# A two-layer attention and pooling step on one core: all low parts of weights on VectorE, layer 1's V tile behind the u tiles, new planner costs, queries by halves

## The chip, the cores and the metric

The kernel runs on one core of one Trainium2 chip. The metric is the device time of one execution in microseconds. A core has five engines that work side by side, each through its own queue of instructions in order: TensorE (PE) for matmuls and transposes, VectorE (DVE), ScalarE (ACT), GpSimd (POOL), and SyncE (SP), whose queue starts all transfers between memory and the on-chip buffer. An instruction that needs another engine's result waits for a semaphore, and what stands behind it in the same queue waits with it.

## The reference: one step of two layers

1152 tokens (128 context, 1024 latent) of width 1024 go through two layers. Each normalises and modulates the tokens, projects them with one matrix of width 2304, feeds a branch of windowed attention (8 query heads, 2 key and value heads) and a branch of pooling, gates both, and projects back into the residual. Results are the tokens after a last normalisation, and the context's keys and values.

```python
h = _rmsnorm(x, norm_w) * (1.0 + scale) + shift
p = h @ w_in
q, k, v, ga, u, gp = split(p)
# latent tokens: q = _rope_2d(q), k = _rope_2d(k); keys within 128 positions and all cached keys
s = jnp.einsum("bqkgd,bnkd->bkgqn", qb, k) * (HEAD_DIM ** -0.5)
m = jnp.maximum(jnp.max(s, -1), sink); e = jnp.exp(s - m)
p = e / (jnp.sum(e, -1) + jnp.exp(sink - m));  attn = p @ v
# pooling: four groups, means over windows of 2, 4, 8, 16, minus the token, then a 128 x 128 map
a = _rmsnorm(attn, attn_norm) * silu(ga);  pl = _rmsnorm(pool, pool_norm) * silu(gp)
x = x + gate * (concat(a, pl) @ w_out)
```

## The kernel before, in words

Tokens lie along the free dimension, in three groups of 384 (G0 to G2; the first 128 of G0 are the context). Channels lie in tiles of 128 partitions. Values that have to be exact to more than one pass of the matrix unit are split: a high part (a rounding copy) and a low part (value minus high part). So a *job* of the input projection, one tile of 128 output channels for one group, is 24 matmuls of 128 x 384: for each of 8 channel tiles weight high by h high, weight high by h low, weight low by h high (`project`). There are 18 such column tiles in a layer (4 q, K, V, 4 gates ga, 4 u, 4 gates gp) and 8 of the output projection, which are loaded twice, once for groups 0 and 1 (pass 1) and once for group 2. That makes 68 column tiles of weights.

Weights come in halves of 256 KB on SP (`wload`), into two raw buffers (`wr`, in the output projection's second pass parts of the tile R). `wsplit` then makes each half's high part on ScalarE and its low part on GpSimd, except for the first three tiles (`WDVE`) and the first half of each tile of the second pass, which are VectorE's. The results lie in two tiles `wh`; the next tile is split when all three groups of the one two before it have been multiplied.

The order within a layer is a list: u0, u1, V, u2, u3, K, q0 to q3, gp0 to gp3, ga0 to ga3, the same in both layers. Layer 0 runs the first three tiles of it as six lanes while its inputs arrive; layer 1 runs the first two for groups 0 and 1, then for group 2, then the rest tile by tile. Two PSUM accumulators (`acc`) take the jobs in turn, and each is evacuated by a routine of its kind. `evac_u` copies u into R, two u tiles at a time, where VectorE forms moving sums (`pool_group`); u2 may be written only when the sums of u0 are done, u3 after u1. When the sums of all four are done, SP loads the tables of cosines and sines over the same place of R (`pool_mix`), and these are needed by the rope of K and q (`evac_k`, `rope`). `evac_v` transposes V and splits it.

Attention runs as two lanes over 18 units (9 blocks of 128 queries, 2 key heads). A unit copies its four heads into the tile `qs` (high parts: heads 0 and 2 from the lower, heads 1 and 3 from the upper partitions, each also to the other half of partitions), subtracts for `ql` (low parts), multiplies with the stacked keys into PSUM tiles `pst`, takes row maxima on VectorE into `s`, exponentials on ScalarE, scales by 1/sum on GpSimd, transposes on TensorE, splits the result in `pth` (ScalarE) and `ptl` (VectorE) and multiplies with V into `pv`. The jobs of the later column tiles are run in between.

The order in each queue is no engine's choice at run time: a planner (`Sched`) runs the kernel's routines as generators against a model of time, always steps the ready routine of the highest priority, and issues instructions in that order. `Engine.cost` and `Tensor.matmul` say what an instruction is planned to take, `LAT` what a result needs to be seen by another engine, and `ready` and `commit` keep when each region of a tile was last written and read. The lines of the profile L111, L137, L148 and L160 are those of the helpers through which every instruction goes (engines, matmul, transpose, DMA), so groups are told apart by tile names.

## Time and profile before

| | us |
|---|---|
| median of 3 runs (range) | 972.14 (969.76 to 972.52) |
| the profiled execution | 972.32 |
| its span, first to last instruction | 970.5 |
| TensorE, VectorE, ScalarE, GpSimd busy | 919.0, 710.6, 533.1, 404.2 |
| mean granted TensorE clock, share of full | 0.993 |

The span is what the trace covers; the execution's own time has 1.8 us more around it. Busy is the time in which an engine has an instruction in work; a matmul's record overlaps the next one's, since they are pipelined. Start times in the views are counted from the span's start.

### The profile page before, as it was taken

To read this page: it belongs to the slowest core of one execution; us is meant where nothing else is said; L and a number is where in the kernel's file an instruction comes from. 1 tells how busy PE (TensorE), PEld (TensorE's weight loads), DVE (VectorE), ACT (ScalarE), POOL (GpSimd) and SP (SyncE) were. 2 spreads that over 40 slices of the span, in tenths; PEclk is the share of its full clock that TensorE was granted. 3 is DMA by queue.
4 is the path that set the end of the run, shared out by engine and by line. 5 is a ranking of instruction groups with operands and counts; after the bars stand their busy time and mean duration, and the time that the engine had idled before them with its cause. 6 is when DMAs were issued, how large, how long until landed. Compare 5 with 4: busy or idle time off the path is not lost.

```text
span 970.5 us, 15980 instructions
## 1 busy us (share of the span) xinstructions
PE 919.0 (95%) x5576; PEld 853.9 (88%) x5576; DVE 710.6 (73%) x1629; ACT 533.1 (55%) x1279; POOL 404.2 (42%) x419
## 2 busy tenths in 40 slices
PE   6899999999999999999989998999999999899995
PEld 2677787999999998899989998988999999899995
DVE  4876567788887569866797466888897776985675
ACT  3453334457766677653455433446776657875442
POOL 2142246663343354345333323776345326434331
PEclk9999999999999999999999999999999999999998
DMA  9714775010000010335431202000000001213463
GB/s 350 296 55 158 233 252 193 23 39 29 22 23 23 23 32 18 120 112 182 169 125 57 75 25 89 23 33 33 24 22 23 23 23 45 71 49 104 137 201 136
DMA packets 42560, 89.02 MB, mean 92 GB/s; under 512 B 4976, under 2 KB 7664, under 8 KB 42480
## 3 DMA queue, kind: packets, MB, share of 16 engines
q1 hardware_dynamic: 42480, 88.00, 26.4%
q8 instruction: 44, 0.72, 0.3%
q14 instruction: 36, 0.29, 0.1%
HBM read 78.28 MB, written 9.70 MB: 91 GB/s over the span
## 4 chain that ended last, share of the span: by engine, by line
PE 69%; DVE 18%; issue 5%; POOL 3%; ACT 3%; DMA 1%; SPq 0%; POOLq 0%; DVEq 0%; ACTq 0%
PE acc L137 46%; PE pst L137 10%; PE pst L148 7%; PE pv L137 6%; DVE G L111 5%; DVE H L111 3%; DVE t L111 2%; DVE R L111 2%; DVE s L111 2%; ACT s L111 1%; DVE ql L111 1%; DMA G<-in_xT 1%; POOL wh L111 1%; DVE den L111 1%; POOL t L111 1%
## 5 line engine op out<-in xcount | busy, mean ns | idle before, releaser
L137 PE MATMUL acc<-H,wh 128*128 128x384 f32 x3624 | 689.9, 339 | 16.2 <-DVE H L111 9.8
L137 PEld LDWEIGHTS acc<-H,wh 128*128 128x128 f32 x3624 | 633.1, 189 | 42.9 <-DVE H L111 12.2
L111 POOL TENSOR_TENSOR wh<-wr,wh 128x512 fp32r<-128x512 f32 x98 | 134.6, 1386 | 174.3 <-ACT wh L111 165.9
L111 POOL TENSOR_SCALAR s<-s,den 128x512 f32<-128x512 f32 (+2 forms) x144 | 105.3, 746 | 140.3 <-DVE den L111 76.9
L111 DVE TENSOR_TENSOR ptl<-pst,pth 128x512 fp32r<-128x512 f32 x124 | 82.4, 686 | 24.1 <-PE pv L137 14.3
L111 DVE CUSTOM_DVE_ANT_0 s<-pst,cst 128x512 f32<-128x512 f32 (+2 forms) x144 | 84.5, 613 | 13.3 <-PE pst L137 12.7
L111 ACT ACTIVATE s<-s,m 128x512 f32<-128x512 f32 (+2 forms) x144 | 93.9, 655 | 0.6
L111 ACT CAST wh<-wr 128x512 fp32r<-128x512 f32 x100 | 61.0, 616 | 54.9 <-PE acc L137 38.8
L111 ACT CAST pth<-pst 128x512 fp32r<-128x512 f32 x124 | 69.2, 585 | 32.5 <-PE pst L148 21.2
L148 PE MATMUL pst<-cst,s 128*128 128x128 f32 x504 | 70.5, 274 | 6.9 <-POOL s L111 5.3
L148 PEld LDWEIGHTS pst<-cst,s 128*128 128x128 f32 x504 | 59.3, 140 | 14.1 <-POOL s L111 8.9
L137 PE MATMUL pst<-K,ql 128*128 128x256 f32 x272 | 69.2, 283 | 1.0 <-DVE ql L111 0.9
L137 PE MATMUL pst<-K,qs 128*128 128x256 f32 x272 | 69.2, 283 | 0.0
L111 ACT ACTIVATE t<-G 128x384 f32<-128x384 f32 x86 | 43.7, 520 | 44.0 <-DVE G L111 28.1
L111 DVE TENSOR_TENSOR R<-R 128x384 f32<-128x384 f32 (+13 forms) x60 | 43.3, 722 | 25.9 <-ACT R L111 24.5
L111 ACT CAST qs<-G 64x256 fp32r<-64x256 f32 x144 | 58.2, 404 | 2.6
L111 DVE SCALAR_TENSOR_TENSOR G<-acc,mods,G 128x384 f32<-128x384 f32 (+2 forms) x64 | 31.5, 512 | 33.8 <-PE acc L137 33.5
L137 PEld LDWEIGHTS pst<-K,ql 128*128 128x128 f32 x272 | 51.3, 189 | 3.4 <-DVE ql L111 1.8
L137 PEld LDWEIGHTS pst<-K,qs 128*128 128x128 f32 x272 | 51.4, 189 | 0.3
L137 PE MATMUL pv<-ptl,V 128*128 128x512 f32 x124 | 50.2, 419 | 0.0
L111 POOL TENSOR_TENSOR rr<-rr,nhalf 128x3 f32<-128x3 f32 x21 | 21.5, 1026 | 68.6 <-DVE rr L111 68.3
L111 ACT COPY t<-pv 64x256 f32<-64x256 f32 x72 | 23.2, 369 | 47.0 <-PE pv L137 46.2
(125 smaller groups left out, 1206.2 us busy)
## 6 DMA issues: line engine op xcount, KB each, us to landing
wr<-in_wi SPq DMA_DIRECT2D x68, 256.0 KB, 2.6
s<-in_wada SPq DMA_DIRECT2D x44, 256.0 KB, 4.3
wr<-in_wo SPq DMA_DIRECT2D x32, 256.0 KB, 2.7
R<-in_wo SPq DMA_DIRECT2D x32, 256.0 KB, 3.8
wk<-in_wada SPq DMA_DIRECT2D x12, 512.0 KB, 7.8
G<-in_xT SPq DMA_DIRECT2D x6, 768.0 KB, 9.5
G<-in_xT SPq DMA_DIRECT2D x12, 384.0 KB, 3.9
xs<-G SPq DMA_DIRECT2D x12, 384.0 KB, 2.4
```

Of the source, the lines that this page charges most:

```text
L111: r = f(*args, **kw)
L137: self.eng.matmul(out, lhsT, rhs, start=start, stop=stop)
L148: self.eng.transpose(out, in_, ident)
```

## The change

Four things, all in the program that builds the kernel; the numbers computed are the same.

- `WDVE` becomes all tiles, so every low part of a weight is VectorE's: 114 halves move there from GpSimd.
- Layer 1 gets an order of its own: u0, u1, u2, u3, V, K, ... Layer 0 keeps its own.
- The planner's costs change: other durations by operation and operand, a time after the end until the result counts as written (`TAIL`, `DRAIN`), less `LAT` on top, a cost for switching between matmuls, transposes and matmuls on 32 columns, 35 ns between dependent instructions of one engine, and a port: GpSimd instructions, and VectorE instructions without a PSUM operand, are not planned at the same time.
- In `qs` and `ql` the two middle dimensions change places: heads 0 and 2 are now one contiguous half, heads 1 and 3 the other.

```diff
@@ -91,18 +91,35 @@
         self.sched, self.eng, self.name = sched, eng, name
         self.free = 0.0
 
+    TAIL = dict(act=105, dve=82, pool=45)
+    HOLD = dict(dve=50, pool=95)
+
     def cost(self, op, n, args, kw):
+        aps = [x for x in list(args) + list(kw.values()) if isinstance(x, bass.AP)]
+        psum = any(x.space == bass.MemoryType.PSUM for x in aps)
+        column = any(free_size(x) == 1 for x in aps if x is not args[0] and x is not kw.get("accum_out"))
         if self.name == "act":
-            return (205 if "accum_out" in kw else 107) + 0.763 * n
-        if self.name == "dve":
+            c = 280 + 0.83 * n if "accum_out" in kw else (80 + 0.755 * n if psum else 73 + 0.855 * n) + 100 * column
+        elif self.name == "dve":
             if op == "reciprocal":
-                return 70 + 6.6 * n
-            if op == "tensor_scalar" and not any(isinstance(x, bass.AP) and x.space == bass.MemoryType.PSUM for x in args):
-                return 70 + 0.52 * n
-            return 70 + 1.04 * n
-        if op == "tensor_tensor" and kw.get("op") == ALU.pow:
-            return 400 + 165 * n
-        return 70 + {"tensor_tensor": 2.35, "scalar_tensor_tensor": 1.46}.get(op, 1.2) * n
+                c = 70 + 6.6 * n
+            elif op == "tensor_reduce":
+                c = 50 + 1.05 * free_size(aps[1])
+            elif op == "memset":
+                c = 15 + 0.52 * n
+            elif op == "tensor_scalar" and not psum:
+                c = 80 + 0.52 * n
+            elif op == "stream_shuffle":
+                c = 190 + 1.05 * n
+            else:
+                c = 65 + 1.05 * n + (62 if column and op == "scalar_tensor_tensor" else 0)
+        elif kw.get("op") == ALU.pow:
+            c = 360 + 165 * n
+        elif op == "tensor_tensor":
+            c = 138 + 2.165 * n
+        else:
+            c = 225 + 0.865 * n
+        return c, self.name == "pool" or self.name == "dve" and not psum and op != "memset"
 
     def __getattr__(self, op):
         f = getattr(self.eng, op)
@@ -114,9 +131,14 @@
             ins += [v for k, v in kw.items() if isinstance(v, bass.AP) and k not in self.OUTS]
             s = self.sched
             start = max(self.free, s.clock, s.ready(ins, outs, self.name))
-            self.free = start + self.cost(op, free_size(args[0]), args, kw)
-            s.commit(ins, outs, self.free, self.name)
-            s.step_end = max(s.step_end, self.free + s.LAT)
+            c, port = self.cost(op, free_size(args[0]), args, kw)
+            if port:
+                start = max([start] + [t for n, t in s.port.items() if n != self.name])
+                s.port[self.name] = start + c + self.TAIL[self.name] - self.HOLD[self.name] - 85
+            self.free = start + c
+            end = self.free + self.TAIL[self.name]
+            s.commit(ins, outs, end, self.name)
+            s.step_end = max(s.step_end, end + s.LAT)
             return r
         return call
 
@@ -124,29 +146,39 @@
 class Tensor:
     def __init__(self, sched, eng):
         self.sched, self.eng = sched, eng
-
-    def issue(self, ins, out, c):
+        self.mode, self.cols = "mm", {}
+
+    DRAIN = 165
+
+    def issue(self, ins, out, c, mode="mm"):
         s = self.sched
-        start = max(s.clock, s.ready(ins, [out], "pe"))
+        start = max(s.clock, s.ready(ins, [out], "pe") - 60)
         s.stall += start - s.clock
-        s.clock = start + c
-        s.commit(ins, [out], s.clock + 60, "pe")
-        s.step_end = max(s.step_end, s.clock + 60 + s.LAT)
+        if mode != self.mode:
+            if self.mode == "col":
+                start = max([start] + list(self.cols.values()))
+            start += 110 if "col" in (mode, self.mode) else 85 if self.mode == "tr" else 0
+            self.mode, self.cols = mode, {}
+        if mode == "col":
+            p = span(out)[1]
+            end = max(start, self.cols.get(p, 0.0)) + c
+            self.cols[p], s.clock = end, start + 35
+        else:
+            end = s.clock = start + c
+        s.commit(ins, [out], end + self.DRAIN, "pe")
+        s.step_end = max(s.step_end, end + self.DRAIN + s.LAT)
 
     def matmul(self, out, lhsT, rhs, start, stop):
         self.eng.matmul(out, lhsT, rhs, start=start, stop=stop)
         n = free_size(rhs)
         if rhs.dtype == R32:
-            c = n / 2.39 if n >= 256 else 213
-        elif lhsT.shape[-1] > 32:
-            c = max(n * 4 / 2.4, 426)
+            self.issue([lhsT, rhs], out, max(n / 2.4 + 13, 109))
         else:
-            c = n * 4 / 2.4 / 4
-        self.issue([lhsT, rhs], out, c)
+            self.issue([lhsT, rhs], out, n * 4 / 2.4, "col")
 
     def transpose(self, out, in_, ident):
         self.eng.transpose(out, in_, ident)
-        self.issue([in_], out, 109)
+        self.issue([in_], out, 109, "tr")
 
 
 class Queue:
@@ -170,7 +202,7 @@
 
 
 
-    LAT = 190
+    LAT = 40
 
     def __init__(self):
         self.clock = 0.0
@@ -179,6 +211,7 @@
         self.tasks = []
         self.count = 0
         self.mem = {}
+        self.port = {}
 
     def ready(self, ins, outs, eng):
         t = 0.0
@@ -191,7 +224,7 @@
                         if we != eng:
                             t = max(t, w + self.LAT)
                         elif eng != "pe":
-                            t = max(t, w)
+                            t = max(t, w + 35)
                         if write and re != eng:
                             t = max(t, r + self.LAT)
         return t
@@ -259,7 +292,7 @@
     HPOOL, HPOOL1, TPOOL = ((), (), (1, 3)), (), (0, 1, 2, 3)
     SLACK = 300.0
     HPRIO = 1
-    WDVE = (0, 1, 2)
+    WDVE = range(200)
     PASS1 = (0, 1)
     GA = (0, 1, 2)
     XDVE, XPOOL = ((0, 2), (1, 3), (1,)), ((), (0,), (0, 2))
@@ -979,14 +1012,14 @@
         qh = yield from self.get("qs", [P, 2, 2, P], R32)
         yield from self.claim(f"ql{g}")
         ql = self.ql[g]
-        S_.copy(qh[0:64, :, 0, :], A)
-        S_.copy(qh[64:128, :, 1, :], B)
-        yield
-        S_.copy(qh[64:128, :, 0, :], A)
-        S_.copy(qh[0:64, :, 1, :], B)
+        S_.copy(qh[0:64, 0], A)
+        S_.copy(qh[64:128, 1], B)
+        yield
+        S_.copy(qh[64:128, 0], A)
+        S_.copy(qh[0:64, 1], B)
         rows = slice(0, 64) if g == 0 else slice(64, 128)
-        V_.tensor_tensor(ql[rows, :, 0, :], A, qh[0:64, :, 0, :].bitcast(F32), op=ALU.subtract)
-        V_.tensor_tensor(ql[rows, :, 1, :], B, qh[64:128, :, 1, :].bitcast(F32), op=ALU.subtract)
+        V_.tensor_tensor(ql[rows, 0], A, qh[0:64, 0].bitcast(F32), op=ALU.subtract)
+        V_.tensor_tensor(ql[rows, 1], B, qh[64:128, 1].bitcast(F32), op=ALU.subtract)
         yield
         if tb == 0:
             pairs = [(slice(0, 2), 0)]
@@ -1012,8 +1045,8 @@
             sm.append(self.make("s"))
             ps = yield from self.get("pst")
             for sl, col in pairs:
-                T_.matmul(ps[:, col:col + 256], qh[:, h // 2, h % 2, :], K[:, g, sl, :], start=True, stop=False)
-                T_.matmul(ps[:, col:col + 256], ql[:, h // 2, h % 2, :], K[:, g, sl, :], start=False, stop=True)
+                T_.matmul(ps[:, col:col + 256], qh[:, h % 2, h // 2, :], K[:, g, sl, :], start=True, stop=False)
+                T_.matmul(ps[:, col:col + 256], ql[:, h % 2, h // 2, :], K[:, g, sl, :], start=False, stop=True)
             self.sc.follow(row_max(h, ps, sm[h]), 1)
             yield 0
         self.put("qs", f"ql{g}")
@@ -1181,11 +1214,11 @@
             sc.spawn(self.evac_ga(l, c - COL_GA, g, acc), 0)
         self.flag("job", l, c, g)
 
-    def main(self, order):
+    def main(self, orders):
         sc = self.sc
         i = 0
         self.left = {}
-        for l in range(DEPTH):
+        for l, order in enumerate(orders):
             pos = {c: i + n for n, c in enumerate(order)}
             for c in order:
                 self.left[pos[c]] = NG
@@ -1238,11 +1271,13 @@
 
     def run(self):
         a = self.a
-        order = [COL_U, COL_U + 1, COL_V, COL_U + 2, COL_U + 3, COL_K, 0, 1, 2, 3] + [COL_GP + j for j in range(4)] + [COL_GA + j for j in range(4)]
+        last = [COL_K, 0, 1, 2, 3] + [COL_GP + j for j in range(4)] + [COL_GA + j for j in range(4)]
+        u = [COL_U + j for j in range(4)]
+        orders = [u[:2] + [COL_V] + u[2:] + last, u + [COL_V] + last]
         items = []
-        self.order, self.items = order, items
+        self.order, self.items = orders[0], items
         for l in range(DEPTH):
-            items += [(a["wi"][l, c], None) for c in order]
+            items += [(a["wi"][l, c], None) for c in orders[l]]
             items += [(a["wo"][l, c], None) for c in range(KD)]
             items += [(a["wo"][l, c], l) for c in range(KD)]
         self.tok["wr2"] = [0.0] * 4
@@ -1251,7 +1286,7 @@
         sc.spawn(self.start(), 0)
         sc.spawn(self.wload(items), 1)
         sc.spawn(self.wsplit(items), 0)
-        sc.spawn(self.main(order), 9)
+        sc.spawn(self.main(orders), 9)
         sc.run()
```

## Rows read from the trace of the kernel before

**Rows 1.** The page's first part: busy time of an engine, its share of the span, instructions.

```profile
PE 919.0 (95%) x5576; PEld 853.9 (88%) x5576; DVE 710.6 (73%) x1629; ACT 533.1 (55%) x1279; POOL 404.2 (42%) x419
```

**Rows 2.** The page's fourth part: shares of the span in the chain of work that ended last, by engine.

```profile
PE 69%; DVE 18%; issue 5%; POOL 3%; ACT 3%; DMA 1%; SPq 0%; POOLq 0%; DVEq 0%; ACTq 0%
```

**Rows 3.** The chain of waits in order of time: start, us, what. One long piece of projection matmuls that waited for nothing.

```profile
435.91 32.27 PE acc L137 x186
```

**Rows 4.** The view by stretches of 25 us over the whole span: the stretch and its length, then busy time and instructions (x) of PE, PEld, DVE, ACT and POOL, the granted clock, the DMA share and GB/s.

```profile
0.00:25.00 25.00, 16.01 (x94) 6.18 (x98) 10.81 (x34) 10.08 (x21) 5.60 (x10) 1.00 0.93 352
...
300.00:325.00 25.00, 25.00 (x161) 24.26 (x160) 17.31 (x50) 16.27 (x42) 9.97 (x12) 1.00 0.09 31
...
375.00:400.00 25.00, 21.19 (x128) 19.40 (x128) 24.11 (x54) 20.99 (x53) 13.43 (x12) 1.00 0.27 85
...
475.00:500.00 25.00, 23.67 (x134) 22.49 (x133) 25.00 (x50) 15.62 (x34) 7.93 (x6) 1.00 0.50 168
500.00:525.00 25.00, 22.64 (x130) 21.68 (x129) 21.93 (x43) 13.89 (x32) 9.60 (x9) 1.00 0.24 82
...
575.00:600.00 25.00, 21.79 (x118) 20.82 (x118) 15.80 (x28) 8.92 (x20) 8.68 (x11) 0.97 0.22 77
600.00:625.00 25.00, 23.71 (x132) 22.76 (x132) 21.67 (x35) 11.33 (x26) 17.14 (x16) 0.96 0.10 32
625.00:650.00 25.00, 23.26 (x132) 22.54 (x131) 19.94 (x51) 11.70 (x35) 16.59 (x18) 0.93 0.06 22
...
825.00:850.00 25.00, 22.02 (x135) 20.74 (x135) 24.54 (x60) 20.39 (x52) 12.09 (x10) 1.00 0.21 69
...
950.00:970.50 20.50, 9.59 (x56) 8.81 (x54) 9.56 (x17) 4.46 (x8) 2.14 (x2) 0.84 0.25 97
```

**Rows 5.** The view of one tile, the weight tile wh, over the whole span: operation and count, duration in ns (least, median, most), first and last start, forms.

```profile
L111 POOL TENSOR_TENSOR wh<-wr,wh x98: 1262/1297/1675, 72.9 to 909.2; 128x512 fp32r<-128x512 f32 x98
...
L111 DVE TENSOR_TENSOR wh<-R,wh x16: 671/691/1248, 461.1 to 950.9; 128x512 fp32r<-128x512 f32 x16
L111 POOL TENSOR_TENSOR wh<-R,wh x16: 1280/1302/1752, 461.7 to 951.6; 128x512 fp32r<-128x512 f32 x16
```

**Rows 6.** Timelines of PE, of the DMA queue SP and of VectorE around the start of layer 1's K tile: start, us, engine, line, operation, and in brackets the idle time before it with what ended it.

```profile
597.20 6.00 PE L137 MATMUL acc<-H,wh 128*128 128x384 f32 x24 [2.19 <-ACT t L111]
603.43 4.46 PE L137 MATMUL acc<-H,wh 128*128 128x384 f32 x24 [0.23 <-ACT t L111]
608.71 6.01 PE L137 MATMUL acc<-H,wh 128*128 128x384 f32 x33 [0.82 <-ACT G L111]
...
583.43 5.87 SPq L160 DMA_DIRECT2D R<-in_cs  x2
...
592.67 0.43 DVE L111 TENSOR_TENSOR t<-t,R 128x256 f32<-128x256 f32 x1 [2.15 <-DMA R<-in_cs]
```

**Rows 7.** The view by chosen stretches, same columns as rows 4.

```profile
597.00:603.50 6.50, 6.07 (x25) 5.75 (x25) 5.57 (x9) 2.36 (x6) 2.98 (x3) 0.74 0.23 81
...
635.00:640.00 5.00, 4.98 (x21) 4.67 (x21) 3.33 (x5) 1.65 (x4) 3.21 (x4) 0.66 0.15 56
```

**Rows 8.** Timelines of PE, VectorE and GpSimd over the moving sums of layer 1's u tiles.

```profile
568.77 0.45 PE L137 MATMUL pst<-ptl,s 128*128 128x384 f32 x1 [1.35 <-DVE ptl L111]
...
585.13 0.45 PE L137 MATMUL pst<-ptl,s 128*128 128x384 f32 x1 [0.94 <-DVE ptl L111]
...
564.72 3.53 DVE L111 TENSOR_TENSOR R<-R 128x390 f32<-128x390 f32 x3 [1.68 <-ACT R L111]
...
569.22 1.75 DVE L111 TENSOR_TENSOR R<-R 128x390 f32<-128x390 f32 x3
...
564.38 2.86 POOL L111 TENSOR_TENSOR wh<-wr,wh 128x512 fp32r<-128x512 f32 x2 [2.01 <-ACT wh L111]
```

**Rows 9.** The timeline of all engines between 627 and 638 us.

```profile
631.20 1.29 POOL L111 TENSOR_TENSOR wh<-wr,wh 128x512 fp32r<-128x512 f32 x1
...
631.60 1.31 DVE L111 TENSOR_TENSOR t<-t,R 128x384 f32<-128x384 f32 x1
...
634.15 0.94 POOL L111 TENSOR_SCALAR s<-s,den 128x128 f32<-128x128 f32 x2 [0.39 <-DVE rr L111]
...
634.80 0.68 PE L148 MATMUL pst<-cst,s 128*128 128x128 f32 x2 [1.72 <-POOL s L111]
```

**Rows 10.** Timelines of PE and VectorE between 470 and 553 us, and from the view by source line of GpSimd's work between 469 and 512 us one group (columns as rows 5).

```profile
487.87 4.08 PE L137 MATMUL acc<-H,wh 128*128 128x384 f32 x22 [0.77 <-POOL wh L111]
...
503.34 7.21 PE L137 MATMUL acc<-H,wh 128*128 128x384 f32 x40 [1.03 <-POOL wh L111]
...
475.87 1.78 DVE L111 SCALAR_TENSOR_TENSOR H<-G,mods,H 128x128 fp32r<-128x128 f32 x2
...
478.23 0.73 DVE L111 SCALAR_TENSOR_TENSOR H<-G,mods,H 128x128 fp32r<-128x128 f32 x2
...
L111 POOL TENSOR_TENSOR wh<-R,wh x7: 1281/1518/1752, 471.1 to 501.8; 128x512 fp32r<-128x512 f32 x7
```

**Rows 11.** The view of waits over the span: who waited for whom, us in total, times, longest.

```profile
POOL wh L111 <- ACT wh L111: 204.6, 47, 19.0
...
ACT wh L111 <- PE acc L137: 63.9, 28, 4.7
```

**Rows 12.** The view by groups, shapes apart: busy us, mean ns of one, idle before it and what ended it.

```profile
L137 PEld LDWEIGHTS pst<-K,ql 128*128 128x128 f32 x272 | 51.3, 189 | 3.4 <-DVE ql L111 1.8
```

## The prediction

> **What bounds the kernel now.** I read the page's busy shares first, then the chain, then the stretches of 25 us, and went from these into the places where TensorE stands. TensorE is busy 95% of the span, VectorE 73%, GpSimd 42% [rows 1]; the chain that ended last is 69% TensorE and 18% VectorE, with 3% each for GpSimd and ScalarE [rows 2]. So most of the time is matmul work that the change doesn't touch. Its pace where nothing is waited for: 186 projection matmuls in 32.27 us, 0.1735 us each [rows 3]. The span is not limited alike everywhere. Through the attention of layer 0 TensorE shows 25.00 of 25 us from 300 to 325 [rows 4], and nothing can be won there. It isn't full in five places: the start, where the DMA share is 0.93; the passage from attention to output projection in both layers (21.19 and 22.02 of 25, VectorE 24.11 and 24.54); the passage to layer 1 (23.67 and 22.64, VectorE 25.00 and 21.93); the head of layer 1 from 575 to 650 (21.79, 23.71, 23.26); and the tail (9.59 of 20.5) [rows 4]. A matmul's record outlasts its pace, so busy time hides short gaps; counting is stricter: 118 instructions from 575 to 600 would need at most 118 x 0.1735 = 20.5 us, so 4.5 us are lost there, and by the same count 2.1 between 600 and 625 and 2.1 between 625 and 650.
>
> The profiled execution took 972.32 us with a span of 970.5, so 1.8 us lie around it; the median shown is 972.14, 0.2 below. I work against 972.3.
>
> **The change part by part.** (1) *Low parts of weights.* There are 136 halves (68 column tiles); 114 of them, 98 and 16 in the tile view, are on GpSimd at a median of 1.30 us, and all go to VectorE, where the same form takes 0.691 [rows 5]. GpSimd loses 98 x 1.297 + 16 x 1.302 = 148 us, VectorE gets 114 x 0.691 = 79 us, which without any relief takes it from 710.6 to 789 us, 81% of the span. Where TensorE is full, VectorE has 17.31 of 25 us taken [rows 4]; two columns in such a stretch add 4 x 0.69 = 2.8 us beside 25 us of matmuls, so I cost this at nothing; if VectorE fell behind by all of it, the 79 us would be the price.
>
> There is relief, because VectorE slows down beside GpSimd. Three moving sums take 1.75 us alone and 3.53 with two low parts on GpSimd beside them [rows 8]; two H low parts take 0.73 alone and 1.78 in the other case [rows 10]. So a low part on GpSimd costs VectorE 0.9 to 1.05 us where VectorE has the matching work, against 0.69 for doing it itself. The Trainium skill (SBUF — State Buffer, Who interferes with whom) says that a VectorE instruction with two SBUF inputs contends with a GpSimd instruction that reads SBUF, and that the loser is blocked for the whole instruction. The trace agrees in size where they overlap (1.05 of an operation of 1.3 us).
>
> Where does this reach TensorE? At the passage to layer 1, seven such parts of the output weights run on GpSimd between 469 and 512 us, and TensorE stands 0.77 and 1.03 us for them [rows 10]. On VectorE, which is full there, each is 1.05 - 0.69 = 0.36 cheaper: 7 x 0.36 = 2.5 us, and the two stalls shrink with the shorter operation, but these overlap. By the counts (134 and 130 instructions) 1.8 + 2.4 = 4.2 us are lost there. I take 2.5; bounds: 4.2 gained, or 7 x 0.69 = 4.8 lost if no relief comes. At the moving sums TensorE stands 1.35 and 0.94 us [rows 8], behind a VectorE chain that two low parts delay by 1.78; if VectorE must do them first it still loses 1.4. Bounds 0 to 2.3, I take 1.2. At 632 us the GpSimd queue is low part, rope product, then the normalisation of s; VectorE's rope product beside it takes 1.31, and the transposes of s wait 1.72 [rows 9]. Right after the stall the granted clock is 0.66 of full on the mean of 5 us [rows 7], so for a part of them it is at 1.2 instead of 2.4 GHz: (1 - 0.66) x 5 = 1.7 us lost. Bounds 0 to 1.7 + 1.7 = 3.4; without the 1.29 us in the queue some 0.4 of the stall is left, so I take 2.5. In the passage from attention to output projection, VectorE is as full; three columns in 25 us bring 6 x 0.69 = 4.1 us and take away at most 6 x 1.05 = 6.3 of blocking. Nearer to nought than to either end: 0, bounds 4 lost to 2 gained in each layer.
>
> (2) *V behind the u tiles in layer 1.* Moved are three jobs of 24 matmuls (12.5 us), their copies, nine transposes, three high and three low parts of V, V's two weight DMAs of 256 KB, now behind the four of u2 and u3 on SP, and the later output of V. In the trace the last moving sums end just before SP's issue of the cosine and sine tables at 583.43, which write over the u tiles; VectorE waits 2.15 us for them at 592.67, the rope of K waits for that, ScalarE's copy of the second accumulator stands behind it, and TensorE stands 2.19, then 0.23 and 0.82 us [rows 6]. The clock is again at the lower level for a part: the 24 matmuls from 597.20 take 6.00 us instead of 4.16 [rows 6, 7]. Together 3.24 + 1.84 = 5.1 us. With V between u3 and K the sums and the tables have 72 matmuls, 12.5 us, as cover, more than the 592.67 - 583.43 = 9.2 us from issue to use. I take the 5.1. What is late next is u2, which now comes right behind u1 and may only be evacuated when the sums of u0 are done: its first job ends two jobs (8.3 us) after u0's last, and three groups of sums with their means are some 4 to 5 us by rows 8; if it doesn't hold, one accumulator wait of 2 to 4 us comes back. Bounds 0 to 5.1. Attention needs V only with K and the queries, 9 jobs later, so nothing waits for V.
>
> (3) *Queries by halves.* Same copies and subtractions, same elements; the matmuls of a head then need two of four copies. All idle time of weight loads before products with ql is 3.4 us, 1.8 of it put down to ql [rows 12]. Bounds 0 to 1.8, taken 0.
>
> (4) *The planner's costs.* They decide only the order in each queue. The old cost of a projection matmul is 384/2.39 = 161 ns, the trace says 173.5; a low part on GpSimd was planned at 70 + 2.35 x 512 = 1273 ns against 1297, and blocking not at all. The new ones are 173 ns, 603 ns for a low part on VectorE, and an exclusion of the two engines. The same plan held to truer costs should wait less, and the waits between engines that it plans shrink, from 190 ns to 62 from VectorE to TensorE (82 + 40 - 60), so it keeps less in hand. The trace can't show this. All idle time of TensorE in rows 1 is 970.5 - 919.0 = 51.5 us; the first 25 and the last 20.5 us hold 9.0 + 10.9 of it, which leaves 31.6. Minus what is taken above, 20 is the upper bound; the lower bound is the third rival. I take 3 us gained, a seventh of it, because most of what is left stands at data that isn't there (DMA, first loads).
>
> Sum: 2.5 + 1.2 + 2.5 + 0 + 5.1 + 0 + 3 = 14.3; 972.3 - 14.3 = 958.0 us. The tail, with TensorE busy for 9.59 of its 20.5 us [rows 4], is taken as unchanged.
>
> **The rivals.** *A: only V's move counts.* VectorE takes over what GpSimd did, and both were the same resource. Then 972.3 - 5.1 = 967 us. For it: VectorE at 25.00 of 25 in one stretch; against: 1.05 blocked against 0.69 worked. The Trainium skill (Perfetto Trace Analysis, Optimizing Scalar/DVE Operations) warns that these two share a read port and that moving work between them might not help; taken strictly that is this rival, and by the two pairs of rows the trace speaks against it. *B: nothing measurable*, 969 to 975: the stalls that go come back one column later, since the same pools of two accumulators and two weight tiles set the pace. For it: TensorE was full for most of the span. *C, slower: VectorE stands at weights that aren't there.* GpSimd waits 204.6 us in 47 waits for ScalarE's cast of wh, ScalarE itself 63.9 us in 28 waits, up to 4.7, for TensorE to free the tile [rows 11]. On GpSimd that held up little; on VectorE the row maxima, the low parts of the probabilities and the evacuations are queued behind it, and TensorE waits for these. If 40% of the 63.9 reaches TensorE it costs 25.6: 972.3 - 14.3 + 25.6 = 984 us. It decides from 14.3 / 63.9 = 22% on. Against it: the planner knows when a tile comes free, and now has TensorE's true pace. *D: the plan gains more*, 10 of the 20 us left: about 950 or less, 947.
>
> **How the numbers follow.** Forecast (950 to 966) 0.48; A (966 to 969) 0.10; D (under 950) 0.12; B 0.14; C 0.16. A change under 0.3%, 2.9 us, can't be told from none. Faster is the forecast, A and D, 0.70; same is B, 0.14; slower is C, 0.16. The range leaves out a third of D and most of C: 943 to 978. Its own range for the forecast alone is 950 to 966.
>
> **What would show it.** No low part on GpSimd, some 250 us busy there, VectorE between 740 and 790; TensorE without the stall at K in layer 1 and the clock at its upper level there; VectorE's H and moving-sum operations near their shortest times; the passage to layer 1 still limited by VectorE. The forecast is wrong if VectorE shows long waits for ScalarE's wh, or if 225 to 375 us is no longer full.

## The result and the profile after

The changed kernel takes 948.7 us (median of 4 runs, 947.9 to 950.0) against 971.6 of the kernel before beside it: ratio 0.9768, 95% interval 0.9748 to 0.9788. The forecast was 958.0 in a range from 943 to 978. The profiled execution took 949.5 us, its span 947.7.

The first and fourth parts of the page after, engines' busy time and shares of the chain:

```profile
PE 914.5 (97%) x5576; PEld 853.1 (90%) x5576; DVE 725.0 (77%) x1743; ACT 533.6 (56%) x1279; POOL 247.6 (26%) x305
...
PE 82%; issue 8%; DVE 4%; ACT 2%; DMA 2%; POOL 1%; SPq 0%; POOLq 0%; DVEq 0%; ACTq 0%
```

Against [rows 1] GpSimd has lost 156.6 us and VectorE gained 14.4, though 79 us of work went there. TensorE's idle time in the span fell from 51.5 to 33.2 us. The chain is now 82% TensorE and 4% VectorE, against 69% and 18% [rows 2]: most of the waits for VectorE on the path are gone.

The stretches of 25 us after (columns as in [rows 4]):

```profile
375.00:400.00 25.00, 21.64 (x124) 19.77 (x124) 23.43 (x63) 17.35 (x46) 1.94 (x3) 0.93 0.27 85
...
475.00:500.00 25.00, 25.00 (x146) 25.00 (x146) 24.11 (x52) 15.73 (x34) 0.00 (x0) 1.00 0.49 165
500.00:525.00 25.00, 23.20 (x132) 22.15 (x131) 19.50 (x46) 12.48 (x28) 4.09 (x4) 1.00 0.12 37
...
575.00:600.00 25.00, 23.72 (x138) 23.02 (x138) 21.79 (x37) 10.00 (x22) 14.91 (x13) 1.00 0.07 25
600.00:625.00 25.00, 25.00 (x152) 24.80 (x152) 21.25 (x48) 11.54 (x33) 18.27 (x19) 1.00 0.13 43
625.00:650.00 25.00, 25.00 (x156) 24.67 (x155) 22.14 (x58) 12.68 (x32) 8.01 (x9) 1.00 0.13 43
...
825.00:850.00 25.00, 24.73 (x138) 22.49 (x137) 21.66 (x50) 17.28 (x43) 4.46 (x5) 1.00 0.28 94
...
925.00:947.70 22.70, 11.75 (x64) 10.65 (x62) 10.63 (x21) 4.47 (x8) 0.85 (x1) 0.76 0.29 113
```

The passage to layer 1 is full up to 500 us and still lacks 1.8 us up to 525. From 600 to 650 us, where 1.29 and 1.74 us were idle [rows 4], TensorE is full. One passage out of attention still stands (375 to 400, 21.64 of 25), the other (825 to 850) hardly. The tail, 925 to the end, is what it was.

The low parts in the view of the tile wh, and the view of waits, after:

```profile
L128 DVE TENSOR_TENSOR wh<-wr,wh x100: 675/691/1511, 12.9 to 884.7; 128x512 fp32r<-128x512 f32 x100
...
L128 DVE TENSOR_TENSOR wh<-R,wh x32: 682/686/694, 453.9 to 928.5; 128x512 fp32r<-128x512 f32 x32
```

```profile
ACT wh L128 <- PE acc L172: 83.5, 39, 4.6
...
DVE wh L128 <- ACT wh L128: 29.6, 27, 4.8
```

All are on VectorE at a median of 0.69 us, as in [rows 5]. VectorE now stands 29.6 us for ScalarE's cast, and ScalarE 83.5 instead of 63.9 us [rows 11] for TensorE to free the tile. So the wait of rival C is there. It hardly reaches TensorE: VectorE's whole share of the chain is 4%, and among those that the view of the tile wh lists as waiting for it there is no projection matmul.

The head of layer 1 in the timelines of SP, VectorE and TensorE after:

```profile
559.68 8.34 SPq L192 DMA_DIRECT2D R<-in_cs  x2
...
574.70 0.45 DVE L128 STREAM_SHUFFLE t<-t 128x256 f32<-128x256 f32 x1
...
583.36 8.08 PE L172 MATMUL acc<-H,wh 128*128 128x384 f32 x45
592.71 3.42 PE L172 MATMUL acc<-H,wh 128*128 128x384 f32 x18 [1.28 <-ACT G L128]
```

The two transfers of the tables are issued between 559.68 and 568.02 us (the row joins both), and K's first rope begins at 574.70, right when ScalarE has copied the accumulator; before, it waited 2.15 us for the tables and TensorE 2.19 us [rows 6], since the second transfer was issued only then:

```profile
588.98 0.33 SPq L160 DMA_DIRECT2D R<-in_cs  x1
```

One stall, 1.28 us, is left at 592.71, further back in the ropes.

The stretch 375 to 400 us shows a wait that wasn't there before. ScalarE and TensorE, timeline after:

```profile
376.12 1.74 ACT L128 CAST H<-G 128x384 fp32r<-128x384 f32 x4
...
378.71 0.62 ACT L128 CAST wh<-wr 128x512 fp32r<-128x512 f32 x1
379.24 0.92 ACT L128 CAST H<-G 128x384 fp32r<-128x384 f32 x2
...
380.06 0.57 ACT L128 CAST pth<-pst 128x512 fp32r<-128x512 f32 x1
...
380.69 1.69 PE L172 MATMUL pv<-pth,V 128*128 128x512 f32 x2 [3.23 <-ACT pth L128]
```

TensorE stands 3.23 us for `pth`, which lies in ScalarE's queue behind casts of H, of queries and of a weight; the granted clock of this stretch is 0.93.

### The profile page after: what moved, and what is told of

It is laid out like the page before. It is cut to its first block, busy times and chain, and to the rows that moved or that the text cites. A ratio compares the mean times of both kernels' runs of the same rounds, so it can differ in the third digit from the quotient of the medians.

```text
span 947.7 us, 16039 instructions
## 1 busy us (share of the span) xinstructions
PE 914.5 (97%) x5576; PEld 853.1 (90%) x5576; DVE 725.0 (77%) x1743; ACT 533.6 (56%) x1279; POOL 247.6 (26%) x305
## 4 chain that ended last, share of the span: by engine, by line
PE 82%; issue 8%; DVE 4%; ACT 2%; DMA 2%; POOL 1%; SPq 0%; POOLq 0%; DVEq 0%; ACTq 0%
PE acc L172 56%; PE pst L172 12%; PE pst L180 7%; PE pv L172 7%; DVE G L128 1%; POOL rr L128 1%; DMA R<-in_cs 1%; DMA ptl<-in_wada 1%; DVE H L128 1%; DVE t L128 1%; DMA G<-in_xT 1%; ACT wh L128 0%; ACT s L128 0%; DVE wh L128 0%; DVE s L128 0%
## 5 line engine op out<-in xcount | busy, mean ns | idle before, releaser
L172 PE MATMUL acc<-H,wh 128*128 128x384 f32 x3624 | 682.3, 338 | 3.6 <-DVE H L128 1.6
L128 DVE TENSOR_TENSOR wh<-wr,wh 128x512 fp32r<-128x512 f32 x100 | 73.0, 739 | 29.7 <-ACT wh L128 26.9
L128 DVE CUSTOM_DVE_ANT_0 s<-pst,cst 128x512 f32<-128x512 f32 (+2 forms) x144 | 84.2, 611 | 13.2 <-PE pst L172 11.3
L172 PE MATMUL pv<-pth,V 128*128 128x512 f32 x124 | 50.6, 425 | 3.5 <-ACT pth L128 3.4
L128 POOL TENSOR_TENSOR G<-G,rb 128x384 f32<-128x384 f32 x40 | 44.3, 1138 | 23.0 <-ACT rb L128 23.0
```

The costliest lines, as they stand in the source:

```text
L128: r = f(*args, **kw)
L172: self.eng.matmul(out, lhsT, rhs, start=start, stop=stop)
```

## The experiments

**The parts alone.** Four kernels, each the kernel before with one part of the change (three dots stand for further lines of the same edit).

```diff
# b_dve
-    WDVE = (0, 1, 2)
+    WDVE = range(200)
# b_order
+        orders = [u[:2] + [COL_V] + u[2:] + last, u + [COL_V] + last]
...
# b_plan
+    TAIL = dict(act=105, dve=82, pool=45)
+    HOLD = dict(dve=50, pool=95)
...
-    LAT = 190
+    LAT = 40
...
# b_half
-        S_.copy(qh[0:64, :, 0, :], A)
+        S_.copy(qh[0:64, 0], A)
...
```

> The kernel before with only the low parts of weights moved to VectorE (old planner costs, old order, old query tiles). My terms: 2.5 + 1.2 + 2.5 = 6 us gained, so 965 us, with VectorE's stretched operations relieved and the stall behind GpSimd at 632 us gone. Rival A (both engines are one resource): 970 to 973 us. Rival C (VectorE stands at weights that are not there yet, since the old planner takes TensorE for 8% faster than it is): 975 us or more, with long waits of VectorE for ScalarE's cast of wh.

> The kernel before with only layer 1's V tile behind the u tiles. My term: 5.1 us gained, so 967 us, the stall of 2.2 us at the start of K in layer 1 gone and no fall of the granted clock behind it. If the stall only moves to the u tiles that now follow each other: 971 to 973 us.

> The kernel before with only the planner's new costs; every instruction is the same, only its place in the queue is another. My term: 3 us gained, so 969 us. If the planner carries most of the 22.8 us: 960 us or less. If its shorter waits between engines leave TensorE nothing in hand without the other parts: 975 us or more.

> The kernel before with only the queries' tiles in halves. My term: 0, at most 1.8 us gained: 970 to 972 us. If the four copies were a wait on the path: 968 us or less.

**The parts taken away.** Three kernels, each the changed kernel with one of these edits reversed (the query halves stay in all three).

```diff
# a_nodve
-    WDVE = range(200)
+    WDVE = (0, 1, 2)
# a_noorder
-        orders = [u[:2] + [COL_V] + u[2:] + last, u + [COL_V] + last]
...
# a_noplan
-    LAT = 40
+    LAT = 190
...
```

> The changed kernel with the low parts of weights back on GpSimd (new planner, new order, new query tiles stay). Alone the move was worth 15.3 us. If the parts add up: 948.7 + 15.3 = 964 us. If the new planner's port rule and the new order already avoid the blocking: 955 us or less. VectorE's time lost to stretched operations should be near 100 us again if blocking is the cause.

> The changed kernel with layer 1 in the old order. Alone the order was worth 10.5 us. If the parts add up: 959 us. If moving the low parts to VectorE already shortens the moving sums so that the tables come in time: 951 us or less.

> The changed kernel with the planner's old costs. Alone the planner was worth 4.3 us. If it adds up: 953 us. If the three gains overlap (15.3 + 10.5 + 4.3 = 30.1 alone, 22.8 together) because the planner's is the part that is had anyway: 947 to 950 us.

Measured, each with the kernel before beside it:

| kernel | low parts on VectorE | V behind u | new planner | us | before | ratio (95% interval) |
|---|---|---|---|---|---|---|
| b_dve | x | | | 957.0 | 972.4 | 0.9846 (0.9831 to 0.9861) |
| b_order | | x | | 961.8 | 972.4 | 0.9890 (0.9875 to 0.9905) |
| b_plan | | | x | 968.0 | 972.4 | 0.9961 (0.9947 to 0.9975) |
| b_half (queries only) | | | | 971.9 | 972.4 | 1.0001 (0.9989 to 1.0013) |
| a_noplan | x | x | | 952.0 | 971.2 | 0.9794 (0.9775 to 0.9813) |
| a_noorder | x | | x | 958.6 | 971.2 | 0.9864 (0.9841 to 0.9887) |
| a_nodve | | x | x | 951.4 | 971.2 | 0.9788 (0.9772 to 0.9804) |
| the change | x | x | x | 948.7 | 971.6 | 0.9768 (0.9748 to 0.9788) |

Alone, the move is worth 1.54%, the order 1.10, the planner 0.39, the query halves nothing that can be measured. That sums to 3.03%, and together they give 2.32. The table says which overlap. The move adds 1.54% to the old kernel, 0.96 where the new order is there already (0.9890 to 0.9794), 0.97 where the planner is (0.9961 to 0.9864), and only 0.20 where both are (0.9788 to 0.9768), which is inside the intervals. The order adds 1.10% to the old kernel and 0.96 to the other two together (0.9864 to 0.9768), but 0.52 to the move alone (0.9846 to 0.9794) and 1.73 to the planner alone (0.9961 to 0.9788). And the new planner added to the move alone gives nothing (0.9846 to 0.9864), but added to the new order 1.02% (0.9890 to 0.9788). So the move overlaps with the order as well as with the planner, while the order and the planner help each other.

The 0.20% don't mean that the planner has repaired what the move repairs. The passage to layer 1 and the passage out of attention, in the stretches of a_nodve:

```profile
375.00:400.00 25.00, 24.90 (x146) 22.87 (x147) 22.81 (x55) 22.67 (x59) 7.96 (x10) 1.00 0.15 45
...
500.00:525.00 25.00, 21.05 (x106) 19.79 (x106) 22.99 (x49) 13.73 (x30) 6.25 (x6) 0.86 0.14 44
```

Without the move the passage to layer 1 still stands: 106 instructions at a granted clock of 0.86, against 132 in the changed kernel, 26 x 0.1735 = 4.5 us. Between 375 and 400 us it is the other way, 146 against 124, since a_nodve doesn't have the wait for `pth`. The 2.7 us between the two kernels are what is left of a gain in one place and a loss in another, and not a measure of what the move repairs. VectorE's lost time is back in a_nodve, as expected: 714.6 us busy with the low parts on GpSimd, 710.6 in the kernel before.

The start shows a gain that no part has alone. The first 300 us of the kernel before, b_dve, b_plan and the changed kernel, in this order:

```profile
0.00:300.00 300.00, 280.34 (x1746) 237.97 (x1747) 215.12 (x515) 156.31 (x380) 128.78 (x144) 1.00 0.39 135
0.00:300.00 300.00, 278.61 (x1730) 238.09 (x1731) 220.39 (x541) 154.65 (x378) 93.61 (x115) 0.99 0.39 135
0.00:300.00 300.00, 281.38 (x1749) 239.45 (x1750) 213.84 (x499) 150.72 (x368) 125.07 (x141) 0.99 0.39 137
0.00:300.00 300.00, 286.53 (x1788) 245.76 (x1789) 217.06 (x543) 155.11 (x379) 96.01 (x119) 0.99 0.39 137
```

TensorE gets through 1788 instructions there instead of 1746, while the move alone makes it 1730 and the planner alone 1749. At 161 in 25 us [rows 4] the 42 more are some 6 us of the 22.8.

Of b_dve the page's busy line, two of its stretches, and the longest waits of TensorE at K and at the normalisation of s in layer 1:

```profile
PE 913.4 (96%) x5576; PEld 854.9 (90%) x5576; DVE 730.5 (76%) x1743; ACT 533.8 (56%) x1279; POOL 245.6 (26%) x305
```

```profile
475.00:500.00 25.00, 25.00 (x147) 24.96 (x146) 25.00 (x58) 16.39 (x38) 0.58 (x1) 1.00 0.55 185
500.00:525.00 25.00, 25.00 (x148) 24.92 (x147) 22.95 (x52) 14.15 (x32) 2.95 (x4) 1.00 0.23 67
```

```profile
590.47 4.46 PE L137 MATMUL acc<-H,wh 128*128 128x384 f32 x24 [2.15 <-ACT t L111]
...
627.57 0.33 PE L148 MATMUL pst<-cst,s 128*128 128x128 f32 x1 [1.24 <-POOL s L111]
```

VectorE is busy for 730.5 us where 710.6 + 79 would be 790: taking 114 low parts off GpSimd gave back 59 us, 0.52 us for each. Between 475 and 525 TensorE is full with 295 instructions instead of 264 [rows 4], 31 x 0.1735 = 5.4 us more work in the same time, while VectorE is still as busy there (25.00 and 22.95 of 25). The two stalls shown last are still there, so the wait behind GpSimd at 632 us, which I expected to be gone, is not.

The two passages out of attention, 100 us around each, before and then in b_dve:

```profile
350.00:450.00 100.00, 95.99 (x588) 91.80 (x587) 79.11 (x179) 62.52 (x153) 47.16 (x45) 1.00 0.24 82
780.00:880.00 100.00, 96.10 (x597) 91.39 (x596) 80.19 (x195) 69.14 (x171) 38.64 (x39) 1.00 0.16 54
```

```profile
350.00:450.00 100.00, 98.60 (x594) 94.89 (x593) 76.83 (x185) 59.10 (x142) 24.11 (x30) 1.00 0.29 94
780.00:880.00 100.00, 100.00 (x614) 97.61 (x613) 82.24 (x199) 65.74 (x160) 25.65 (x30) 1.00 0.19 62
```

TensorE's idle time there falls by 2.6 and 3.9 us.

Of b_order the stretches, and the longest wait of TensorE between 560 and 650 us:

```profile
575.00:600.00 25.00, 24.76 (x147) 24.37 (x146) 15.04 (x26) 11.79 (x26) 15.01 (x14) 1.00 0.19 56
600.00:625.00 25.00, 24.07 (x144) 23.38 (x143) 22.08 (x41) 10.83 (x25) 22.23 (x19) 1.00 0.12 33
625.00:650.00 25.00, 24.27 (x146) 22.92 (x145) 20.57 (x52) 13.84 (x42) 15.93 (x19) 1.00 0.14 43
```

```profile
606.60 0.55 PE L148 MATMUL pst<-cst,pre 128*128 128x128 f32 x3 [0.93 <-POOL pre L111]
```

Against [rows 4] 147 instead of 118 instructions go through TensorE between 575 and 600 us, then 144 and 146 instead of 132 and 132: the gain isn't the stall at K alone but reaches over the next 50 us. The mean granted clock is 1.00 in all three, instead of 0.97, 0.96 and 0.93. With the stall at K, those at the moving sums [rows 8] and the one at 634.80 [rows 9] are gone too; five short ones are left, 1.8 us in all.

**Blocking, or a slow engine?** Two kernels keep b_dve's queues on all engines but GpSimd, which gets unused work at the places where the low parts were (the tile `junk` and the change of `WDVE` as in b_dve are left out here).

```diff
# d_tt
+                if i > 2 and not (second is not None and h == 0):
+                    hi = parts[0][h].bitcast(F32)
+                    self.nc.gpsimd.tensor_tensor(self.junk, hi, hi, op=ALU.subtract)
# d_ms
+                if i > 2 and not (second is not None and h == 0):
+                    for _ in range(2):
+                        self.nc.gpsimd.memset(self.junk, 0.0)
```

> The kernel of b_dve (957.0 us), and at each of the 114 places GpSimd makes an unused subtraction of the same size, two inputs in the buffer, after the same wait as the low part had; nobody waits for its result. If what made the low parts on GpSimd dear was that VectorE is blocked beside them: 970 us or more, since VectorE now has the 79 us of work and the blocking. If it was that the low parts came late from a slow engine: 957 to 960 us.

> The kernel of b_dve (957.0 us) with two unused fills of a tile on GpSimd at each of the 114 places where d_tt had a subtraction: they hold GpSimd's queue for a comparable time but read nothing from the buffer. The subtractions brought 37 us (994.2). If those came from VectorE being blocked by GpSimd's reads: 957 to 962 us here, and VectorE's time lost to stretched operations near b_dve's 63 us. If they came from GpSimd's own queue (normalisations, ropes and roots of rows standing behind): 985 us or more.

Measured: d_tt 994.2 us, ratio 1.0229 (1.0212 to 1.0246); d_ms 965.8, ratio 0.9932 (0.9909 to 0.9954). The busy lines of d_tt and of d_ms:

```profile
PE 925.9 (93%) x5576; PEld 858.4 (87%) x5576; DVE 795.9 (80%) x1743; ACT 534.7 (54%) x1279; POOL 393.2 (40%) x419
```

```profile
PE 922.5 (95%) x5576; PEld 859.4 (89%) x5576; DVE 734.1 (76%) x1743; ACT 534.4 (55%) x1279; POOL 359.4 (37%) x533
```

A subtraction whose result nobody reads makes VectorE, with the same instructions, 65.4 us busier than in b_dve (795.9 against 730.5), 0.57 us for each of the 114; the fills add 3.6. So in this pair GpSimd's subtraction, which reads its inputs in the buffer, blocks VectorE, and its filling, which reads nothing, doesn't. The passage to layer 1 shows what that does to TensorE; its stretch in d_tt and then in d_ms, and a wait of TensorE in d_tt:

```profile
500.00:525.00 25.00, 20.09 (x110) 18.84 (x109) 25.00 (x42) 12.45 (x24) 7.60 (x7) 0.96 0.44 146
```

```profile
500.00:525.00 25.00, 25.00 (x148) 24.93 (x147) 24.17 (x55) 15.79 (x35) 1.98 (x2) 1.00 0.26 84
```

```profile
524.02 0.88 PE L148 MATMUL pst<-cst,R 128*128 128x128 f32 x3 [3.75 <-DVE R L111]
```

With the subtractions VectorE is full there with 42 instructions and TensorE stands 3.75 us for it; with the fills TensorE is full. The 37 us between b_dve and d_tt are not all blocking, though. The fills cost 8.8 of them too (965.8 lies between the two expectations), so holding GpSimd's queue has a price of its own. And d_tt's subtractions, unlike the fills, wait for ScalarE's cast, 147.8 us in 51 waits, which holds the queue longer, and ScalarE's next casts into `wh` wait 3.5 us in all until they have read it. How the remaining 28 divide between blocking and these waits was not separated over the whole kernel.

**Where the move pays.**

```diff
-    WDVE = (0, 1, 2)
+    WDVE = (0, 1, 2) + tuple(range(18, 34)) + tuple(range(52, 68))
```

> The kernel before with the low parts of the output projection's weights alone on VectorE (32 tiles of 68, 48 of the 114 moved halves). If the 9 us by which I undervalued the move lie in the passages out of attention and into layer 1, which run on output weights: 960 to 963 us. If they lie at the head of layer 1, with its input weights: 967 us or more.

Measured 965.1 us, ratio 0.9927 (0.9900 to 0.9953), between the two expectations: 7.1 us of the 15 come with the output weights' 48 halves, and the other 8, by difference, with the 66 of the input weights. My undervaluing was not confined to the passages.

**Which of the planner's costs?**

```diff
-            if port:
+            if False:
                 start = max([start] + [t for n, t in s.port.items() if n != self.name])
```

> The kernel of a_nodve (951.4 us: low parts on GpSimd, new order, new planner) with the planner's port rule alone taken out; the other new costs stay. If that rule is why the planner makes the move to VectorE nearly superfluous (2.7 us instead of 15.3): 960 us or more. If it is the truer durations and the truer times between engines: 949 to 954 us.

Measured 988.9 us, ratio 1.0165 (1.0143 to 1.0186): 37.5 us slower than a_nodve, and slower than the kernel before, though the better order of layer 1 is in it. Busy line and chain of a_nodve, then of op_noport:

```profile
PE 915.6 (96%) x5576; PEld 853.1 (90%) x5576; DVE 714.6 (75%) x1629; ACT 535.2 (56%) x1279; POOL 394.1 (41%) x419
...
PE 81%; DVE 6%; issue 4%; ACT 4%; DMA 2%; POOL 1%; SPq 0%; POOLq 0%; DVEq 0%; ACTq 0%
```

```profile
PE 924.8 (94%) x5576; PEld 851.8 (86%) x5576; DVE 718.1 (73%) x1629; ACT 537.9 (54%) x1279; POOL 399.2 (40%) x419
...
PE 61%; DVE 20%; issue 7%; POOL 5%; ACT 4%; DMA 2%; SPq 0%; POOLq 0%; DVEq 0%; ACTq 0%
```

VectorE and GpSimd are busy for nearly the same time in both (714.6 and 718.1, 394.1 and 399.2 us), so the port rule doesn't lessen the blocking as a whole. What changes is how much of it TensorE meets: the chain is 81% TensorE with the rule and 61% without, with VectorE's share going from 6 to 20%. Without the rule the new costs are no gain but a loss: b_order, with the old costs, the new order and its low parts on GpSimd too, takes 961.8 us. The new costs hold truer durations and shorter waits between engines, and which of the two does the harm was not tried; nor was the rule taken out of a kernel with all low parts on VectorE.

**A version that beats both.** With the new costs the planner's own total follows the chip: 943.3, 944.0, 954.5 and 969.6 us for kernels measured at 948.7, 951.4, 958.6 and 968.0. So I let it choose among its settings and column orders.

```diff
-    NORM_POOL = (0, 1, 2, 3)
+    NORM_POOL = (0, 1, 3)
-    TP, MP, HP0 = 1, 1, 1
-    HPOOL, HPOOL1, TPOOL = ((), (), (1, 3)), (), (0, 1, 2, 3)
-    SLACK = 300.0
-    HPRIO = 1
+    TP, MP, HP0 = 2, 1, 1
+    HPOOL, HPOOL1, TPOOL = ((), (), ()), (), (0, 1, 2, 3)
+    SLACK = 500.0
+    HPRIO = 0
-        orders = [u[:2] + [COL_V] + u[2:] + last, u + [COL_V] + last]
+        orders = [u[:2] + [5, 12, 13, 4, 0, 1, 2, 3, 16, 17, 15, 14, 7, 6, 9, 8], [10, 11, 12, 13, 5, 0, 1, 2, 4, 3, 14, 15, 17, 16, 6, 8, 9, 7]]
```

> The changed kernel with four settings of the planner changed and some columns permuted, chosen by the planner's own total, which is 921.4 us for it and 943.3 for the changed kernel (944.0, 954.5 and 969.6 for a_nodve, a_noorder and b_plan, measured at 951.4, 958.6 and 968.0). If that total says where the chip goes: 925 to 938 us. If the ranking held only among near copies: 945 us or more.

Measured 937.2 us, ratio 0.9634 (0.9616 to 0.9653): faster than the changed kernel by 1.4%. Among its settings are two more pieces of work taken from GpSimd for VectorE (a quarter of the normalisations, four tiles of H). Its stretches:

```profile
375.00:400.00 25.00, 25.00 (x147) 24.09 (x146) 22.62 (x51) 19.07 (x46) 2.71 (x4) 1.00 0.32 95
...
500.00:525.00 25.00, 24.80 (x145) 24.78 (x145) 19.11 (x43) 14.02 (x30) 3.35 (x8) 1.00 0.15 48
...
575.00:600.00 25.00, 25.00 (x149) 24.89 (x148) 20.16 (x33) 8.96 (x21) 18.21 (x16) 1.00 0.14 43
600.00:625.00 25.00, 25.00 (x150) 24.92 (x150) 18.74 (x46) 10.77 (x26) 12.40 (x11) 1.00 0.14 45
```

The stretches that still stood in the changed kernel (375 to 400, 500 to 525, 575 to 600) are full or nearly so. How much of the 1.4% is the order and how much is the work taken from GpSimd was not separated. Its planned total is 15.8 us under the chip's; with a_nodve it was 7.4 under, with b_plan 1.6 over. The ranking held, the size did not. That one rule of the planner is worth nearly 4% also says how to read the smaller steps of the table above: a part changes the order of the queues everywhere, and each step is one such order against another.

## Why the prediction was right, and where not

The direction and the range held, and so did two mechanisms: low parts on GpSimd block VectorE, and V behind the u tiles covers the tables. The sizes did not: 958.0 was forecast and 948.7 measured, 14.3 against 22.8 us gained. The result lies below the forecast's own bracket (950 to 966), in that of rival D, the plan that gains more, and the range held it only because it took in most of D: that is luck, since D's reason is not what the runs show. (Its terms also give 972.3 - 11.3 - 10 = 951 us, and not 947.) The planner is worth 4.3 us alone and 0.26% on top of the rest (0.9794 to 0.9768). Step by step:

- *Low parts of weights, 2.5 + 1.2 + 2.5 = 6.2 us.* Mis-sized: alone they bring 15.3 us. The blocking itself was well read: 0.9 to 1.05 us from two pairs of rows, where VectorE has the matching work, against 0.52 to 0.57 as a mean over all 114 in b_dve and d_tt. What failed is the step from VectorE to TensorE. I counted the stalls that [rows 8 to 10] name and put the passages out of attention at nought: they give 2.6 and 3.9 us, and the passage to layer 1 gives 5.4 instead of 2.5, more than the 4.2 that I had as its bound. (A transpose counted as a projection matmul makes that bound somewhat low.) How much of this is blocking longer than I took it and how much low parts that come sooner was not separated. Of the 2.5 us for the wait at 632 us only the fall of the clock went: b_dve still stands 1.24 us there, at a granted clock of 1.00.
- *V behind u, 5.1 us.* Mis-sized by half: 10.5 alone, 0.96% on top of the other two, 0.52% on top of the move alone. The stall at K went as I worked out, and the sums and tables had their cover; u2 right behind u1 cost nothing that shows. What I had wrong is to which part the stalls next to it belong. In b_order the stalls at the moving sums (1.35 + 0.94 us) and the one at 634.80 (1.72) are gone as well, and so are the falls of the clock, (0.03 + 0.04 + 0.07) x 25 = 3.5 us. With the 3.24 us at K that is 10.8 us, less 1.8 in new short stalls: most of the 10.5. I had put the sums and the wait at 632 under the move. The move alone takes the stalls at the sums and the second fall of the clock away too, which fits with the order being worth less beside it. One reading was off: the row at 583.43 [rows 6] joins two transfers, of which the second was issued at 588.98, after the last sums. From there to the use are 3.7 us and not 9.2, so the cover that the tables need once the sums are done is smaller than I took it.
- *Queries by halves, 0.* Right.
- *The planner, 3 us.* The size was right (4.3 alone), the reason was not. I had it from truer durations and shorter waits; op_noport shows that the new costs without the port rule are 27 us worse than the old ones (988.9 against b_order's 961.8), so the gain hangs on the port rule. Nor is it an addend: it is worth 1.02% to a kernel that has the new order and its low parts on GpSimd, and nothing to one with the move alone. And the 6 us in the first 300, which the change has and neither the move nor the planner has alone, stand in no term.
- *The sum.* I added the terms. Two were half their size or less, the parts overlap (30.1 us alone, 22.8 together), and these errors went opposite ways: that the sum came within 10 us is in part luck.
- *Rival A* (VectorE and GpSimd are one resource, so only the order counts, 967 us) falls as a statement on the old planner: b_dve alone gains 15 us. Beside the new order and planner the move's net worth is 0.20%, inside the intervals, but as the sum of a gain in the passage to layer 1 and a loss elsewhere. So the warning of the Trainium skill (Perfetto Trace Analysis, Optimizing Scalar/DVE Operations), that moving work between these two might not help, is not borne out by the trace of b_dve (15.3 us gained), and the 2.7 us between a_nodve and the changed kernel neither bear it out nor speak against it.
- *Rival C* (VectorE at weights that aren't there): its waits appeared, 29.6 us, the longest 4.8, and decided nothing.
- *What would show it:* VectorE was put at 740 to 790 us and shows 725, since it got back more than I counted; GpSimd at about 250 and shows 247.6. TensorE is full from 225 to 375 us (25.00 in each of the six stretches), so of the two signs of being wrong the second stayed away, and the first, waits for ScalarE's wh, came without harm.

## What to carry to other kernels

When two engines block each other, count what the busier one gets back, not only what it takes on, and look for the gain wherever that engine is full, not only at the stalls that name the other: 79 us of added work became 20. If a program orders the queues, give it the blocking as a rule; here, in one pair of kernels, that was worth 37 us, and the new costs without it were worse than the old ones. Measure the parts of a change alone and against the rest, and then look at the stretches: a part that gained 1.5% alone was worth 0.2% beside the others, and that was a gain in one place less a loss in another.

## What was not expected of the hardware

Work on GpSimd whose result nobody reads lengthened this kernel by 37 us out of 957: a subtraction with its inputs in the buffer cost VectorE 0.57 us for each of 114, a fill 0.03 for each pair. And two kernels with the same instructions, and VectorE and GpSimd busy for nearly the same time (714.6 and 718.1, 394.1 and 399.2 us), lie 37 us apart by the order of the queues alone.
